# Out-projection ended pair by pair with its weights taken four times, the second product's first loads in idle pages of the x ring, and unit 0's splits placed step by step

## Chip, cores and metric

The kernel runs on one NeuronCore of a Trainium2 chip. The metric is the device time of one execution in microseconds, lower is better. TensorE does the matmuls and transposes, VectorE (DVE) and ScalarE (ACT) the elementwise work, GpSimd (POOL) a few small operations, and SyncE's queue (SP) issues the transfers named here.

## What is computed

A trunk of two layers over 1024 tokens of width 1024. Each layer is a token mixer with a norm and a residual, then a SwiGLU feed-forward with inner width 2816, again with norm and residual. Both parts are wrapped in RMS norms. The mixers (an mLSTM with memory attention in layer 0, sliding-window attention with memory attention in layer 1) are not touched by the change.

```python
def swiglu(h, w_in, w_out):
    gate, up = jnp.split(h @ w_in, 2, axis=-1)
    return (jax.nn.silu(gate) * up) @ w_out

for l in range(DEPTH):
    ...
    mix = jnp.concatenate([main, mo], axis=-1) @ w_out[l]
    x = x + rmsnorm(mix, g_mix_post[l])
    x = x + rmsnorm(swiglu(rmsnorm(x, g_ffn_pre[l]), w_ffn_in[l], w_ffn_out[l]), g_ffn_post[l])
```

## The kernel before

All large products are of float32 accuracy, from three matmuls of reduced operands each. An operand v is split into hi, a rounded copy that ScalarE makes (a cast), and lo = v - hi, which VectorE makes; the product is hi by hi, hi by lo, lo by hi. So each tile of weights costs a load (256 KB for 128x512), a cast and a subtraction before TensorE can use it. The helper `mm` (L177) records every matmul, so almost all matmuls stand under that line; transposes are L184.

**Out-projection** (class `OutProjection`, L500 to 555). The 1024 tokens are eight tiles of 128. `tiles(n, ts)` makes half n (512 columns) of the product for the tiles ts, 8 rows of weights deep; `weights(n)` takes the half's weights into the ring of hi and lo parts (8 buffers of each, raw parts in a ring of 4; L206 to L217). The two halves alternate, since the ring holds one half's weights and a new take fills it as the old one is read: half 0 for tiles 0, 4 and 1, 5, then half 1 for all tiles in pairs, then half 0 again for 2, 6, then 3 and 7 alone. So three takes a layer. A half product is squared on ScalarE for its norm (L242) and multiplied by the gain on VectorE into y (L520). When a tile has both halves, `finish` (L467 to 494) runs as side work: load of the residual xr (L471), sum of squares, r, one scalar_tensor_tensor (STT, L484) that adds the residual, the store of y (L486), squares, a second r, and xn = y * r on ScalarE (L494). Then `absorb` (L317 to 342) transposes xn on TensorE into PSUM, copies it to f (L324), and, when the second tile of a pair (t and t + 4) is there, makes sums sx, sy and splits them into parts named a22, s1, s3 (a11 was made by the first tile).

**First product of the feed-forward** (`ffn_in`). Units (p, g): 11 pairs p of 256 columns, for gate (g = 0) and up (g = 1). Each unit is one 2x2 block product with seven multiplications, Strassen's way: seven steps, each with an operand of the tokens (a11, s1, ...) and one of the weights (b11, t1, ...), summed into three PSUM chains u, c, d. `prep` (L608, L609) splits one weight operand, `evict` (L679 to L704) takes the results out of PSUM, `side` places the splits and loads of the unit that comes next. Unit 0 is done in two halves, for tiles 0, 4, 1, 5 and then 2, 6, 3, 7, since the tokens arrive late; all of its seven weight operands are split ahead of its first half. `operands` (L713 to L725) stores the unit's results, and sums sx and sy of them, to DRAM as the spill `sp`.

**Second product** (`ffn_out`): the same seven steps with 11 pairs each, 77 loads of a token operand from `sp` (L785) and a weight operand (L791) into pages, each split by L799 (cast) and L800 (lo). Loads of steps 0 and 1 stand in the raw ring, of the others in the x ring, which has 5 pages of 128x1024. The generator is entered once, by `then()` after ffn_in's last unit (L762).

**What sets the order.** The elementwise order of VectorE, ScalarE and GpSimd in this stretch is that in which the program records it (a manual schedule). A modelled clock, `line.poll`, decides after which matmul the next piece of side work (`finish`, `absorb`) is recorded. TensorE's and SyncE's orders are set by the scheduler; a queue runs strictly in its order, so an instruction that waits holds up all behind it.

## Time and profile before

| | us |
|---|---|
| median of 3 runs | 2196.94 (2193.93 to 2198.35) |
| the profiled execution's own time | 2195.92 |
| its span in the profile | 2194.1 |
| mean granted TensorE clock | 0.984 of full speed |

The profile is one execution. In it PE is TensorE, DVE VectorE, ACT ScalarE. A timeline row is start, duration and instruction in the form out<-in, and in brackets the time that the engine was idle before it, with what ended the wait. Durations overlap on one engine, so the distance of starts tells how fast a queue goes. Names: po is the out-projection's PSUM tile; fgu, fgc, fgd (gate) and fuu, fuc, fud (up) the first product's chains; fou, foc, fod the second's; pt_mix holds transposes; wout, b11g, t1g and so on are weight operands; so the second product's operands; gx, gy, ux, uy the units' results.

### The profile page before, as it was taken

To read this page: it belongs to the slowest core of one execution; us is meant where nothing else is said; L and a number is where in the kernel's file an instruction comes from. 1 tells how busy PE (TensorE), PEld (TensorE's weight loads), DVE (VectorE), ACT (ScalarE), POOL (GpSimd) and SP (SyncE) were. 2 spreads that over 40 slices of the span, in tenths; PEclk is the share of its full clock that TensorE was granted. 3 is DMA by queue.
4 is the path that set the end of the run, shared out by engine and by line. 5 is a ranking of instruction groups with operands and counts; after the bars stand their busy time and mean duration, and the time that the engine had idled before them with its cause. 6 is when DMAs were issued, how large, how long until landed. Compare 5 with 4: busy or idle time off the path is not lost.

```text
span 2194.1 us, 30716 instructions
## 1 busy us (share of the span) xinstructions
PE 2103.6 (96%) x11011; PEld 1809.0 (82%) x11011; DVE 1284.1 (59%) x2462; ACT 1126.1 (51%) x2429; POOL 131.1 (6%) x245
## 2 busy tenths in 40 slices
PE   7999997989999999899999999999899999989997
PEld 6899986877888888688888998988788888878886
DVE  6331247576675757565585347747757676655556
ACT  5541145576555555344474426647655554534444
POOL 1100032000000000000021021000000000000002
PEclk9999998999999999999999999999999999999998
DMA  6111152253454535466672112025245454447666
GB/s 217 54 30 34 50 172 70 87 173 111 148 171 136 184 134 171 165 216 202 193 251 89 41 35 78 2 78 172 94 138 183 138 171 161 141 155 234 194 192 230
DMA packets 174841, 301.34 MB, mean 137 GB/s; under 512 B 20544, under 2 KB 78432, under 8 KB 174688
## 3 DMA queue, kind: packets, MB, share of 16 engines
q1 hardware_dynamic: 174688, 299.38, 42.0%
q8 instruction: 86, 1.41, 0.3%
q14 instruction: 67, 0.55, 0.1%
HBM read 215.94 MB, written 83.38 MB: 136 GB/s over the span
## 4 chain that ended last, share of the span: by engine, by line
PE 79%; issue 10%; DVE 4%; ACT 3%; DMA 2%; POOL 1%; SPq 0%; POOLq 0%; ACTq 0%; DVEq 0%
PE fuu L177 11%; PE fgu L177 10%; PE fou L177 10%; PE po L177 8%; PE fud L177 5%; PE fod L177 5%; PE fgd L177 5%; PE pb_q L177 3%; PE foc L177 3%; PE fuc L177 3%; PE fgc L177 2%; PE pa_ogm L177 2%; PE pov L177 2%; PE pt_mix L184 1%; PE pb_mq L177 1%
## 5 line engine op out<-in xcount | busy, mean ns | idle before, releaser
L800 DVE TENSOR_TENSOR so_lo<-so,so_hi 128x512 fp32r<-128x512 f32 x300 | 195.9, 689 | 172.9 <-ACT so_hi L799 172.7
L799 ACT CAST so_hi<-so 128x512 fp32r<-128x512 f32 x300 | 173.8, 619 | 211.2 <-PE fou L177 82.3
L177 PE MATMUL po<-wout_hi,f 128*128 128x512 f32 x512 | 161.8, 394 | 6.3 <-DVE f L258 6.3
L177 PE MATMUL fou<-so_hi,so_hi 128*128 128x512 f32 x352 | 138.3, 396 | 11.1 <-ACT so_hi L799 11.1
L177 PE MATMUL fou<-so_lo,so_hi 128*128 128x512 f32 x352 | 138.9, 395 | 3.6 <-DVE so_lo L800 3.6
L177 PE MATMUL fou<-so_hi,so_lo 128*128 128x512 f32 x352 | 138.4, 393 | 0.0
L236 POOL TENSOR_TENSOR r<-v,neghalf 128x1 f32<-128x1 f32 (+1 forms) x76 | 55.9, 746 | 1167.5 <-DVE v L234 977.4
L177 PEld LDWEIGHTS po<-wout_hi,f 128*128 128x128 f32 x512 | 97.1, 190 | 26.6 <-DVE f L258 6.6
L177 PE MATMUL po<-wout_lo,f 128*128 128x512 f32 x256 | 100.5, 393 | 0.0
L177 PEld LDWEIGHTS fou<-so_hi,so_hi 128*128 128x128 f32 x352 | 67.0, 190 | 25.8 <-ACT so_hi L799 11.9
L177 PEld LDWEIGHTS fou<-so_lo,so_hi 128*128 128x128 f32 x352 | 67.0, 190 | 18.9 <-DVE so_lo L800 5.3
L177 PEld LDWEIGHTS fou<-so_hi,so_lo 128*128 128x128 f32 x352 | 66.9, 190 | 13.9
L609 DVE TENSOR_TENSOR t1u_lo<-wu,t1u_hi 128x512 fp32r<-128x512 f32 x22 | 15.2, 692 | 101.6 <-ACT t1u_hi L608 101.6
L598 ACT ACTIVATE wu<-wu,gin 128x256 f32<-128x256 f32 x176 | 73.5, 499 | 1.6 <-DMA wu<-in_w_ffn_in 1.5
L598 ACT ACTIVATE wg<-wg,gin 128x256 f32<-128x256 f32 x176 | 73.2, 499 | 0.0
L177 PE MATMUL pb_q<-w_q_hi,h 128*128 128x384 f32 x256 | 72.4, 346 | 0.0
L177 PE MATMUL fod<-so_hi,so_lo 128*128 128x512 f32 x176 | 68.5, 389 | 0.0
L177 PE MATMUL fod<-so_lo,so_hi 128*128 128x512 f32 x176 | 68.5, 389 | 0.0
L177 PE MATMUL fod<-so_hi,so_hi 128*128 128x512 f32 x176 | 68.5, 389 | 0.0
L177 PE MATMUL pa_v<-wa_v_hi,h 128*128 128x384 f32 x256 | 65.4, 336 | 0.0
L619 DVE TENSOR_TENSOR wo_raw<-wo_raw,wo_raw 128x512 f32<-128x512 f32 x88 | 60.6, 689 | 1.5
L177 PE MATMUL fgd<-f,t1g_hi 128*128 128x512 f32 (+1 forms) x192 | 56.0, 374 | 2.1 <-DVE f L314 2.1
(445 smaller groups left out, 5806.9 us busy)
## 6 DMA issues: line engine op xcount, KB each, us to landing
so<-sp SPq DMA_DIRECT2D x150, 256.0 KB, 3.0
wg<-in_w_ffn_in SPq DMA_DIRECT2D x44, 512.0 KB, 3.8
wu<-in_w_ffn_in SPq DMA_DIRECT2D x44, 512.0 KB, 4.1
wo_raw<-in_w_ffn_out SPq DMA_DIRECT2D x88, 256.0 KB, 3.4
tp<-wo_raw SPq DMA_DIRECT2D x88, 256.0 KB, 3.1
so<-tp SPq DMA_DIRECT2D x88, 256.0 KB, 3.5
so<-in_w_ffn_out SPq DMA_DIRECT2D x62, 256.0 KB, 3.4
wout_raw<-in_w_out SPq DMA_DIRECT2D x48, 256.0 KB, 3.0
```

The source lines that it names most:

```text
L177: pe.matmul(o, lhsT=lhsT, rhs=rhs, start=start, stop=stop, **kw)
L184: pe.transpose(o, src, ident[: src.shape[0], : src.shape[0]])
L236: pool.tensor_tensor(out=r, in0=v, in1=neghalf[:, :width], op=ALU.pow)
L598: act.activation(v, v, AF.Copy, scale=gin[:, l, 4 * i + k : 4 * i + k + 1])
L609: dve.tensor_tensor(out=lo, in0=v, in1=h.bitcast(F32), op=ALU.subtract)
L619: dve.tensor_tensor(out=r[o], in0=r[x_], in1=r[y_], op=ALU.add)
L799: act.copy(h, v)
L800: dve.tensor_tensor(out=lo, in0=v, in1=h.bitcast(F32), op=ALU.subtract)
```

## The change

Five edits.

1. In `absorb`, the second half of f is copied from PSUM by VectorE instead of ScalarE (L324).
2. The parts of a pair's second tile are made in the order s1, s3, a22, not a22, s1, s3.
3. The out-projection's last pairs: half 1 of tiles 2, 6, then half 0 of 2, 6, which ends that pair; then half 0 of 3, 7, and last half 1 of 3 and of 7. Half 1's weights are taken a second time, so there are four takes a layer.
4. In unit 0, three weight operands are split ahead of it, the others one by one, at steps of its first half.
5. The second product's generator is entered three times within the last unit, behind its steps 4, 5 and 6: loads of steps 0 to 2 first, then split 0 and load 3, then split 1 and load 4. All of its loads go to pages of the x ring.

```diff
@@ -321,7 +321,7 @@
                 for i in range(4):
                     k = 4 * j + i
                     flip(pt[:, i * P : (i + 1) * P], xn[:, k * P : (k + 1) * P])
-                act.copy(f[:, j * 512 : (j + 1) * 512], pt)
+                (dve.tensor_copy if j else act.copy)(f[:, j * 512 : (j + 1) * 512], pt)
             if not second:
                 self.first[slot] = f
                 yield 0.5
@@ -335,11 +335,11 @@
             dve.tensor_tensor(out=sx[:, 512:], in0=sx[:, :512], in1=a11, op=ALU.subtract)
             dve.tensor_tensor(out=sy[:, :512], in0=a11, in1=a21, op=ALU.subtract)
             dve.tensor_tensor(out=sy[:, 512:], in0=a12, in1=sx[:, 512:], op=ALU.add)
-            self.parts(slot, "a22", a22, 1)
-            yield 1
             self.parts(slot, "s1", sx, 2)
             yield 1
             self.parts(slot, "s3", sy, 2)
+            yield 1
+            self.parts(slot, "a22", a22, 1)
 
     def token_gemm(outs, acts, w):
 
@@ -547,12 +547,12 @@
             self.tiles(1, (0, 4))
             mixed(3, 7)
             self.tiles(1, (1, 5))
-            self.tiles(1, (2, 6))
-            self.tiles(1, (3, 7), lambda: self.weights(0))
+            self.tiles(1, (2, 6), lambda: self.weights(0))
+            self.tiles(0, (2, 6))
+            self.tiles(0, (3, 7), lambda: self.weights(1))
             early()
-            self.tiles(0, (2, 6))
             for t in (3, 7):
-                self.tiles(0, (t,))
+                self.tiles(1, (t,))
 
 
 
@@ -734,7 +734,7 @@
         ordered.__enter__()
         for u, (p, g) in enumerate(units):
             if u == 0:
-                for _, op in STEPS:
+                for _, op in STEPS[:3]:
                     prep(0, op)
                 need(xo, (0, 4, 1, 5))
             results(u)
@@ -759,8 +759,11 @@
                         line.poll()
                     if slots[1] == 4:
                         side(u, s)
+                    elif s + 3 < len(STEPS):
+                        prep(0, STEPS[s + 3][1])
                     evict(u, s, acc, c0, c1)
-        then()
+                    if u == len(units) - 1 and s >= 4:
+                        then()
         for s in (0, 4, 6):
             operands(NP - 1, s)
         ordered.__exit__(None, None, None)
@@ -777,11 +780,8 @@
         def load(n):
             s, p = steps[n]
             sop, wop = STEPS[s]
-            if n < 2:
-                r = raws[n] = [raw_part(f"so{l}_{n}_{i}") for i in range(2)]
-            else:
-                x_ = xpage(f"so{l}_{n}")
-                r = raws[n] = [x_[:, i * 512 : (i + 1) * 512] for i in range(2)]
+            x_ = xpage(f"so{l}_{n}")
+            r = raws[n] = [x_[:, i * 512 : (i + 1) * 512] for i in range(2)]
             nc.sync.dma_start(out=r[0], in_=sp[p][:, SP.index(sop)])
             if wop in TP:
                 nc.sync.dma_start(out=r[1], in_=tp_[p][:, TP.index(wop)])
@@ -800,9 +800,14 @@
                 dve.tensor_tensor(out=lo, in0=v, in1=h.bitcast(F32), op=ALU.subtract)
                 parts[n] += [h, lo]
 
-        for n in range(2):
+        for n in range(3):
             load(n)
-            split_parts(n)
+        yield
+        split_parts(0)
+        load(3)
+        yield
+        split_parts(1)
+        load(4)
         yield
         gpost = grow(a["g_ffn_post"][l], f"gfpost{l}")
         nxt = open_acts(name) if name else None
@@ -839,13 +844,12 @@
                 dve.tensor_tensor(out=z[:, lo], in0=v, in1=gpost[:, lo], op=ALU.mult)
                 line.run(finish(z, z, ss[t2], t2, src, spill, nxt, f"ffn{l}", nxt is None), nxt and (nxt.name, t2))
 
-        load(2)
         for n, (s, p) in enumerate(steps):
             name, begin = CHAIN[s]
             if p == 0 and begin:
                 for j in range(4):
                     acc[name, j] = ps(f"fo{name}{l}_{j}")
-            if n + 3 < len(steps):
+            if 5 <= n + 3 < len(steps):
                 load(n + 3)
             ah, al, bh, bl = parts.pop(n)
             for j in range(4):
```

VectorE, from layer 0's last unit of the first product into the second. L696 to L704 finish the unit's results, L716 to L723 are the sums of its operands; so_2_0_lo is step 2's token operand. Before:

```order
L696 TENSOR_TENSOR ux_10_8088<-ux_10_8088,gx_10_7930 128x512 x2
L703 TENSOR_TENSOR uy_10_8089<-fuu_10_8090,gy_10_7931 128x512
L704 TENSOR_TENSOR uy_10_8089<-uy_10_8089,gy_10_7931 128x512
L800 TENSOR_TENSOR so_0_0_lo<-so_0_0_raw,so_0_0_hi 128x512
L800 TENSOR_TENSOR so_0_1_lo<-so_0_1_raw,so_0_1_hi 128x512
L800 TENSOR_TENSOR so_1_0_lo<-so_1_0_raw,so_1_0_hi 128x512
L800 TENSOR_TENSOR so_1_1_lo<-so_1_1_raw,so_1_1_hi 128x512
L716 TENSOR_TENSOR sx_10_8234<-uy_10_8089 128x512
...
L717 TENSOR_TENSOR sx_10_8234<-sx_10_8234,ux_10_8088 128x512
L722 TENSOR_TENSOR sy_10_8237<-ux_10_8088,uy_10_8089 128x512
...
L800 TENSOR_TENSOR so_2_0_lo<-so_2_8268,so_2_0_hi 128x512
L800 TENSOR_TENSOR so_2_1_lo<-so_2_8268,so_2_1_hi 128x512
```

and with the change:

```order
L696 TENSOR_TENSOR ux_10_8136<-ux_10_8136,gx_10_7978 128x512 x2
L800 TENSOR_TENSOR so_0_0_lo<-so_0_8225,so_0_0_hi 128x512
L800 TENSOR_TENSOR so_0_1_lo<-so_0_8225,so_0_1_hi 128x512
L703 TENSOR_TENSOR uy_10_8137<-fuu_10_8138,gy_10_7979 128x512
L704 TENSOR_TENSOR uy_10_8137<-uy_10_8137,gy_10_7979 128x512
L800 TENSOR_TENSOR so_1_0_lo<-so_1_8228,so_1_0_hi 128x512
L800 TENSOR_TENSOR so_1_1_lo<-so_1_8228,so_1_1_hi 128x512
L716 TENSOR_TENSOR sx_10_8289<-uy_10_8137 128x512
L800 TENSOR_TENSOR so_2_0_lo<-so_2_8231,so_2_0_hi 128x512
L717 TENSOR_TENSOR sx_10_8289<-sx_10_8289,ux_10_8136 128x512
L722 TENSOR_TENSOR sy_10_8292<-ux_10_8136,uy_10_8137 128x512
...
L800 TENSOR_TENSOR so_2_1_lo<-so_2_8231,so_2_1_hi 128x512
```

Step 0's two lo now stand ahead of the uy operations, and step 1's behind them; step 2's are mixed with the sums sx and sy, where they stood behind all of them.

SyncE over the same place. L713 to L725 are the stores of a unit's results and sums, sp_10 those of the last pair. Before:

```order
L713 DMA sp_10_4380<-ux_10_8088 128x1024
...
L714 DMA sp_10_4380<-uy_10_8089 128x512
...
L214 DMA w_kv_raw<-in_w_kv 128x512 x2
L721 DMA sp_10_4380<-sx_10_8234 128x1024
L725 DMA sp_10_4380<-sy_10_8237 128x1024
L785 DMA so_2_8268<-sp_2_4372 128x512
L791 DMA so_2_8268<-in_w_ffn_out 128x512
L785 DMA so_3_8275<-sp_3_4373 128x512
```

and with the change, one unit earlier, behind the stores of pair 9:

```order
L721 DMA sp_9_4517<-sx_9_8007 128x1024
L785 DMA so_0_8225<-sp_0_4508 128x512
L791 DMA so_0_8225<-in_w_ffn_out 128x512
L725 DMA sp_9_4517<-sy_9_8096 128x1024
L785 DMA so_1_8228<-sp_1_4509 128x512
L791 DMA so_1_8228<-in_w_ffn_out 128x512
L785 DMA so_2_8231<-sp_2_4510 128x512
L791 DMA so_2_8231<-in_w_ffn_out 128x512
L785 DMA so_3_8257<-sp_3_4511 128x512
L791 DMA so_3_8257<-in_w_ffn_out 128x512
L785 DMA so_4_8284<-sp_4_4512 128x512
L791 DMA so_4_8284<-in_w_ffn_out 128x512
```

The loads of steps 2 to 4 stood behind the stores of sx_10 and sy_10; now all loads up to step 4 stand ahead of every store of pair 10.

VectorE at the end of layer 0's out-projection, where y_3 and y_7 are the last two tiles and b11g_0_lo is what unit 0's first product needs. Before:

```order
L520 TENSOR_TENSOR y_3_4356<-po_0_3_4470,gmp_3632 128x512
...
L609 TENSOR_TENSOR b11g_0_lo<-wg_0_0_4392,b11g_0_hi 128x512
...
L609 TENSOR_TENSOR b21g_0_lo<-wg_0_1_4394,b21g_0_hi 128x512
L609 TENSOR_TENSOR t2g_0_lo<-t_raw,t2g_0_hi 128x512
L609 TENSOR_TENSOR t1g_0_lo<-t_raw,t1g_0_hi 128x512
L609 TENSOR_TENSOR t3g_0_lo<-t_raw,t3g_0_hi 128x512
L609 TENSOR_TENSOR b22g_0_lo<-wg_0_1_4394,b22g_0_hi 128x512
L520 TENSOR_TENSOR y_7_4363<-po_0_7_4513,gmp_3632 128x512
```

and with the change:

```order
L324 COPY f_mix_2_4573<-pt_mix_2_1_4580 128x512
L324 COPY f_mix_6_4586<-pt_mix_6_1_4593 128x512
L334 TENSOR_TENSOR sx_mix_6_4599<-f_mix_6_4586 128x512
L314 TENSOR_TENSOR f_3637<-f_mix_2_4573,f_3637 128x2x512
...
L337 TENSOR_TENSOR sy_mix_6_4600<-f_mix_2_4573,sx_mix_6_4599 128x512
L520 TENSOR_TENSOR y_3_4494<-po_1_3_4550,gmp_3632 128x512
L314 TENSOR_TENSOR f_3637<-sx_mix_6_4599,f_3637 128x2x512
L314 TENSOR_TENSOR f_3637<-sy_mix_6_4600,f_3637 128x2x512
L314 TENSOR_TENSOR f_3637<-f_mix_6_4586,f_3637 128x512
...
L520 TENSOR_TENSOR y_7_4501<-po_1_7_4619,gmp_3632 128x512
...
L609 TENSOR_TENSOR b11g_0_lo<-wg_0_0_4530,b11g_0_hi 128x512
```

b11g_0_lo stood behind y_3's last product and ahead of y_7's. Now it stands behind both, and behind the copies, sums and splits of tiles 2 and 6, which stood behind it. A stretch ahead of these rows, the lo of the fourth take (wout_1_0 to wout_1_7) are new.

## Rows read from the trace of the kernel before

**Rows 1.** The page's line of busy time by engine (us, share of the span, instructions), and the shares of the chain that ended last.

```profile
PE 2103.6 (96%) x11011; PEld 1809.0 (82%) x11011; DVE 1284.1 (59%) x2462; ACT 1126.1 (51%) x2429; POOL 131.1 (6%) x245
...
PE 79%; issue 10%; DVE 4%; ACT 3%; DMA 2%; POOL 1%; SPq 0%; POOLq 0%; ACTq 0%; DVEq 0%
```

**Rows 2.** Windows: stretch (us), its length, busy us and instructions of PE, PEld, DVE, ACT and POOL, granted clock, DMA share, GB/s. The first two are layer 0's out-projection and unit 0, the third its way into the second product; the fourth and fifth are layer 1's unit 0 and its way into the second product.

```profile
376.25:472.35 96.10, 96.10 (x449) 80.37 (x449) 56.97 (x103) 52.92 (x105) 6.90 (x13) 0.98 0.30 101
472.35:511.64 39.29, 29.22 (x205) 27.53 (x203) 25.91 (x41) 30.29 (x56) 2.55 (x3) 0.91 0.34 116
913.90:933.50 19.60, 11.12 (x37) 8.09 (x36) 12.16 (x20) 4.98 (x9) 2.79 (x35) 0.83 0.89 287
1520.40:1559.70 39.30, 29.00 (x203) 27.27 (x203) 25.95 (x41) 30.12 (x55) 2.57 (x3) 0.91 0.31 103
1962.26:1978.85 16.59, 10.40 (x38) 7.58 (x36) 11.01 (x18) 4.98 (x9) 0.00 (x0) 0.90 0.81 283
```

**Rows 3.** Timeline of TensorE over the second product's first steps, layer 0 and, from 1962.26, layer 1: start, duration, instruction, and in brackets the idle time before it and what ended it.

```profile
913.90 1.07 PE L177 MATMUL fou<-so_hi,so_hi 128*128 128x512 f32 x4
...
916.85 0.50 PE L177 MATMUL fou<-so_lo,so_hi 128*128 128x512 f32 x1 [1.88 <-DVE so_lo L800]
...
928.27 0.80 PE L177 MATMUL fou<-so_hi,so_hi 128*128 128x512 f32 x1 [6.60 <-ACT so_hi L799]
...
930.44 0.63 PE L177 MATMUL fou<-so_lo,so_hi 128*128 128x512 f32 x1
...
930.87 0.63 PE L177 MATMUL fou<-so_hi,so_lo 128*128 128x512 f32 x1
...
933.50 0.39 PE L177 MATMUL fou<-so_hi,so_hi 128*128 128x512 f32 x1
...
933.73 0.40 PE L177 MATMUL fou<-so_lo,so_hi 128*128 128x512 f32 x1
...
1962.26 1.07 PE L177 MATMUL fou<-so_hi,so_hi 128*128 128x512 f32 x4
...
1965.01 0.50 PE L177 MATMUL fou<-so_lo,so_hi 128*128 128x512 f32 x1 [1.68 <-DVE so_lo L800]
...
1974.34 0.80 PE L177 MATMUL fou<-so_hi,so_hi 128*128 128x512 f32 x1 [4.50 <-ACT so_hi L799]
...
1978.85 0.40 PE L177 MATMUL fou<-so_hi,so_hi 128*128 128x512 f32 x1
```

**Rows 4.** Timeline of VectorE, SyncE's queue (SPq) and ScalarE in the same stretch of layer 0.

```profile
911.99 1.28 DVE L696 TENSOR_TENSOR ux<-ux,gx 128x512 f32<-128x512 f32 x2
...
914.10 0.69 DVE L703 TENSOR_TENSOR uy<-fuu,gy 128x512 f32<-128x512 f32 x1 [0.83 <-PE fuu L177]
...
914.71 0.68 DVE L704 TENSOR_TENSOR uy<-uy,gy 128x512 f32<-128x512 f32 x1
...
915.31 2.89 DVE L800 TENSOR_TENSOR so_lo<-so_raw,so_hi 128x512 fp32r<-128x512 f32 x4
...
920.18 0.68 DVE L723 TENSOR_TENSOR sy<-ux,sx 128x512 f32<-128x512 f32 x1
...
920.89 0.33 SPq L725 DMA_DIRECT2D sp<-sy  x1
...
921.27 0.99 SPq L785 DMA_DIRECT2D so<-sp  x1
...
926.69 0.62 ACT L799 CAST so_hi<-so 128x512 fp32r<-128x512 f32 x1 [13.51 <-DMA so<-sp]
```

**Rows 5.** The chain that ended last, pieces in order of time (start, us, what), out-projection and unit 0 of layer 0.

```profile
429.53 1.75 PE pt_mix L184 x16
...
494.57 1.05 ACT xn_mix L494
...
495.67 1.54 PE pt_mix L184 x8
...
501.56 3.20 ACT wu L598 x8
```

**Rows 6.** Timeline of TensorE, transposes of unit 0 (x16 are tiles 2 and 6, x8 tile 7).

```profile
478.97 3.58 PE L184 MATMUL pt_mix<-ident,xn_mix 128*128 128x128 f32 x16 [2.15 <-ACT xn_mix L494]
...
495.67 1.52 PE L184 MATMUL pt_mix<-ident,xn_mix 128*128 128x128 f32 x8 [3.87 <-ACT xn_mix L494]
```

**Rows 7.** Timeline of VectorE from the end of the out-projection into unit 0, layer 0.

```profile
469.58 0.69 DVE L609 TENSOR_TENSOR b11g_lo<-wg,b11g_hi 128x512 fp32r<-128x512 f32 x1 [0.36 <-ACT b11g_hi L608]
...
471.75 0.68 DVE L609 TENSOR_TENSOR t2g_lo<-t_raw,t2g_hi 128x512 fp32r<-128x512 f32 x1
...
472.35 0.68 DVE L609 TENSOR_TENSOR t1g_lo<-t_raw,t1g_hi 128x512 fp32r<-128x512 f32 x1
...
475.36 1.28 DVE L484 SCALAR_TENSOR_TENSOR y<-y,r,xr_mix 128x1024 f32<-128x1024 f32 x1
...
488.43 1.22 DVE L314 TENSOR_TENSOR f<-sx_mix,f 128x1024 fp32r<-128x1024 f32 x1
```

**Rows 8.** Timeline of ScalarE, the table load for silu in unit 0, layer 0.

```profile
491.04 1.28 ACT L693 ACT_TABLE_LOAD   x1
```

**Rows 9.** Group of instructions by line and form: count | busy us, mean ns of one | idle before.

```profile
L1387 DVE COPY pT<-pt 128x512 f32<-128x512 f32 x21 | 14.4, 687 | 0.0
```

**Rows 10.** The tile wout_raw, all 48 loads of 256 KB.

```profile
DMA to landing us min/median/max: 2.4/3.0/5.6
```


## Prediction

> **What bounds it now.** The page's busy line and its chain of waits come first: TensorE is busy 96% of the span, and 79% of the chain that ended last is its matmuls [rows 1]. So only places where TensorE waits, or runs at its lower clock, can give time back. The windows show the two kinds of place that the edits touch [rows 2]. While the out-projection runs, TensorE is busy in all of its 96.10 us and VectorE in 56.97. In feed-forward unit 0 (472.35 to 511.64 in layer 0) TensorE is busy 29.22 of 39.29 us, and layer 1's stretch reads the same (29.00 of 39.30). From the last unit into the second product (913.90 to 933.50) it is busy 11.12 of 19.60 us at a granted clock of 0.83; layer 1's loses a little less, at 0.90.
>
> **Into the second product.** TensorE's timeline has it step by step [rows 3]. In layer 0 step 0's first four matmuls start at 913.90. Then it waits 1.88 us for so_lo, and before step 2 it waits 6.60 us for a cast. After that the matmuls stand 0.43 us apart (930.44, 930.87) where later ones stand 0.23 apart (933.50, 933.73): of the clock's two levels the lower, 1.2 GHz, after that idle time. A step is 12 matmuls at 0.227, so 2.72 us, and step 3 could start at 913.90 + 3 x 2.72 = 922.06. It starts at 933.50: 11.4 us lost. Layer 1 waits 1.68 and 4.50 us and starts step 3 at 1978.85 where 1962.26 + 8.16 = 1970.42 was due: 8.4 us lost.
>
> The causes stand on VectorE, ScalarE and SyncE [rows 4]. VectorE can make so_lo (915.31) only after the two uy operations at 914.10 and 914.71. Step 2's load is issued at 921.27, behind the sy store at 920.89, which waits for VectorE's sy (920.18); the cast follows its landing at 926.69.
>
> The change puts steps 0 to 2 into idle pages of the x ring, so SyncE has all the loads up to step 4 ahead of the last unit's stores, a unit of some 30 us earlier. They cost SyncE issue slots in a stretch where it waits on data, and nothing on the path. VectorE now does so_0's two lo ahead of uy: 911.99 + 2 x 0.6 puts them at 913.3 to 914.5, in time. Behind them stand uy twice, so_1's two (the second done at about 917.2, needed at 916.6 + 0.3), sx, so_2's first, three sums, so_2's second. At 0.60 us apart (471.75 to 472.35) [rows 7] the last is done near 921.0, needed near 919.9. I count two waits of 0.3 and 1.1 us, 1.4 a layer, too short to bring the lower clock, as the 1.88 us wait did not. The gain is 11.4 - 1.4 = **10.0** in layer 0 and 8.4 - 1.4 = **7.0** in layer 1. Bounds: nothing left of either loss (19.8), or a second wait as long as layer 0's first in each (16.0 would be left of 19.8 at 1.9 each). What is late next is step 5, which needs the page that so_2's second lo frees: issued about 921, landed by 925, needed at 928.
>
> **Out-projection and unit 0.** TensorE does the same matmuls. The 16 transposes of tiles 2 and 6, 1.75 us [rows 5], move from unit 0 into the out-projection, which ends at 474.1 instead of 472.35, and no longer wait there (2.15 us at 478.97) [rows 6]. That is what the new order buys: pair 2, 6 is finished one pair earlier, so tiles 3 and 7 alone are left behind the last matmul.
>
> It pays with a fourth take of the weights: 8 loads, 8 casts on ScalarE, 8 subtractions on VectorE; ScalarE loses as many f copies (8 a layer), VectorE gains them. A VectorE copy out of PSUM lasts 0.687 us [rows 9], like the other half-width operations. Rows 4 to 7 of this take use buffers that rows 0 to 3 must leave, and their loads stand on SyncE behind the stores of y_2 and y_6, whose STT runs at about 457; so I issue them at 457.7. At the median landing of 3.0 us [rows 10] they land at 460.7, are cast at 461.6 and subtracted at 462.25. TensorE wants row 4 when it reaches tile 3 alone: 474.1 less two tiles of 24 matmuls (5.44 each) and the 1.75 is 461.5, and four rows of 0.68 later is 464.2. So the take is covered by 2 us.
>
> But VectorE has no gap from 461.65: 20 half-width operations (four lo of the take, four t_raw, four y products, two f copies, four sums, and lo of t and f), three full-width lo at 1.2 [rows 7] and small ones, 12.1 + 3.5 + 0.4 = 16.0, stand ahead of and with b11g_lo, which ends at 477.7; before, it started at 469.58. TensorE gets a **new wait of 2.6 us** or so behind the out-projection's last matmul (with no lower clock if it goes as after 2.15 us; after 3.87 us it came, and would cost at most some 2 us, in matmuls whose end then still lies ahead of tile 3's f). From 477.7 tile 7's work queues behind splits: b21, t2, y_3's STT (1.2), t1, t3, gx, b22, y_7's STT, about 7.0 us on VectorE to 484.65; then on ScalarE y_7's square 1.2 and xn_3 1.05 (each a pass over 1,024 columns, as the xn at 494.57), gy 0.3, the table load 1.28 [rows 8], four silu, a copy and a cast 2.7, and xn_7 1.05: 492.25. In the kernel before, xn_7 ends at 495.6 (494.57 + 1.05) [rows 5]. What follows is the same work: transposes, f, sums, casts, the eight gains of wu (3.20 at 501.56), and unit 0's last matmuls, 16 us to 511.64; the copy that VectorE takes and the new order s1, s3, a22 make it shorter by 0.2. So 3.4 + 0.2 = **3.6 us a layer**, 7.2 in all. Bounds: TensorE's whole idle time in unit 0, 10.1 us a layer [rows 2], and, with the loads landing in the longest row's 5.6 us, 1.0.
>
> **Sum.** The profiled execution took 2195.9 us; 2195.9 - 17.0 - 7.2 = 2171.7. The median of the runs lies 1.0 above it, so the prediction is **2172**. About 0.2%, 4.4 us, is what a measurement can tell from no change.
>
> **Rivals.**
> A. The fourth take lands late. For it: its loads wait in SyncE's order for two stores, and the DMA share is 0.30 there, 0.34 in unit 0 with landing times from 2.4 to 5.6 us [rows 2, 10]. Every us past 3.0 moves VectorE's queue, so unit 0 gives 1.0 a layer or slightly less than nothing: 2195.9 - 17.0 - 2.0, so 2177 to 2182. The Trainium skill, "DMA: Bandwidth & Descriptors", adds a mechanism in "Latency and other measured facts": access latency of memory rises from 0.2 us to about 2 us under high load. By that, as an estimate from the page, landing would come 1.8 us later and the total near 2175; the spread of the rows here agrees with a load effect, without saying which of its parts it is.
> B. Unit 0 gives much more. VectorE's queue is as short as I have priced it, but splits that are placed step by step may let y_7's STT and square pass, so that TensorE loses only about 2 of its 10.1 us: 8 a layer, 2195.9 - 17.0 - 16.0 = 2163. Against it: the order of VectorE and ScalarE is fixed as written, and there the splits do stand ahead of tile 7.
> C. The change does not do what it says: the pages are not idle, the early loads wait for their last readers, and the second product still starts late. Then only unit 0's 7.2 is left: 2189. Against it: the pages' last readers are the stores of unit 9's sums, and they stand right ahead of the loads on SyncE.
> D. Slower: tiles 3 and 7 starve. If the take's rows 4 to 7 are held behind the y_6 store, which needs the STT, its r and its xr load, TensorE stops inside the out-projection, where it never waits now. To eat 17.0 this must cost 8.5 a layer after unit 0's gain of 3.6, so 12.1 a layer: the loads would have to land 14 us later than 460.7, with the 2 us of cover. At 16 us a layer, with the lower clock behind it, the total is near 2205. Against it: the longest landing is 5.6 us, and no operation ahead of the store is priced over 1.3.
>
> **Chances.** The forecast (2166 to 2177) has 0.52, A 0.20, B 0.18, C 0.05, D 0.05. A range of 2160 to 2187 holds forecast, A, B and the bounds of the transition, and leaves out C, D and the outer ends: about 0.15. Faster by over 0.2% is all but D and a corner of C: 0.94; within 0.2%: 0.02; slower: 0.04.
>
> **What would show it.** Right: no wait of 4 us or more ahead of fou's first three steps in either layer, that stretch near 9.5 us at clock 1.0 instead of 19.60 and 16.59, step 3 near 922 after its step 0 at 914; the transposes of tiles 2 and 6 inside the out-projection; a new wait of 2 to 3 us ahead of the first fgu, ended by b11g_lo on VectorE; unit 0 from the end of the out-projection's matmuls some 34 us long instead of 39.29. Wrong: a wait of TensorE for wout_lo or wout_hi in the last half products (A, or D if it is long); no wait ahead of the first fgu, or a far shorter unit 0 (B); a wait on so_hi as before (C). A wait further into the second product, at step 5, would be the transition's loss moved on, not removed.

## The result, and the profile after

The changed kernel takes 2184.78 us (median of 5 runs, 2183.79 to 2189.07) against 2196.94: a ratio of 0.995, 95% interval 0.9933 to 0.9968. It is faster, by 12.2 us where 24.9 were forecast. The profiled execution is the longest of the five, 2189.07 us with a span of 2187.3.

The executions differ by some 5 us in stretches that no edit touches (the first out-projection matmul starts at 373.5 to 378.5 us over the profiles of this study), so the stages are compared, each from its own first matmul:

| stretch, us | before | after | after - before |
|---|---|---|---|
| out-projection, layer 0 / 1 | 96.10 / 94.28 | 99.09 / 96.86 | +2.99 / +2.58 |
| unit 0, layer 0 / 1 | 39.29 / 39.46 | 40.74 / 40.49 | +1.45 / +1.03 |
| second product's first matmul to layer 1's input projection (its first pb_mq matmul) | 290.35 | 279.72 | -10.6 |
| second product's first matmul to the end, layer 1 | 218.05 | 210.03 | -8.0 |

So the way into the second product gave 18.6, a little more than forecast, and out-projection with unit 0, forecast to give 3.6 a layer, took 4.4 and 3.6. By the medians the loss is 18.6 - 12.2 = 6.4 over both layers, not 8.0; the stages are those of one execution. (Layer 1's unit 0 ends at 1559.90 in the kernel before; its window in [rows 2] stops 0.2 us short of that.)

Windows of the changed kernel, same columns as [rows 2]: layer 0's out-projection, its unit 0, the second product's first 8.6 us, then layer 1's unit 0 and its second product.

```profile
378.24:477.33 99.09, 98.50 (x465) 81.75 (x465) 65.25 (x116) 58.97 (x113) 8.73 (x12) 0.98 0.37 123
477.33:518.07 40.74, 30.30 (x189) 28.80 (x187) 26.95 (x45) 24.90 (x48) 4.59 (x4) 0.79 0.31 103
920.36:929.00 8.64, 8.29 (x36) 6.24 (x35) 8.64 (x14) 1.74 (x3) 3.07 (x35) 1.00 0.77 210
1520.24:1560.73 40.49, 29.68 (x187) 28.28 (x188) 27.78 (x46) 25.66 (x49) 4.62 (x4) 0.83 0.28 91
1962.97:1971.60 8.63, 8.60 (x38) 6.64 (x37) 8.63 (x15) 1.75 (x3) 0.00 (x0) 1.00 0.58 215
```

The second product now starts at full clock, where [rows 2] had 0.83 and 0.90. Unit 0 is no shorter, and its clock fell from 0.91 to 0.79.

TensorE and SyncE at the second product of the changed kernel, layer 0:

```profile
920.36 0.84 PE L177 MATMUL fou<-so_hi,so_hi 128*128 128x512 f32 x3
...
921.04 0.44 PE L177 MATMUL fou<-so_lo,so_hi 128*128 128x512 f32 x1
...
927.40 0.50 PE L177 MATMUL fou<-so_lo,so_hi 128*128 128x512 f32 x1 [0.35 <-DVE so_lo L800]
```

```profile
886.09 0.42 SPq L785 DMA_DIRECT2D so<-sp  x1
...
895.02 0.32 SPq L725 DMA_DIRECT2D sp<-sy  x1
895.38 0.43 SPq L785 DMA_DIRECT2D so<-sp  x1
...
899.10 0.43 SPq L791 DMA_DIRECT2D so<-in_w_ffn_out  x1
```

Against [rows 3, 4]: the waits of 1.88 and 6.60 are gone, all that is left is 0.35; the loads up to step 4 are issued by 899.5, over 20 us ahead of their use, where step 2's went out 7 us behind step 0's start. In layer 1 no wait is left there.

TensorE in layer 0's unit 0, the rows that answer to [rows 6]:

```profile
480.03 0.50 PE L177 MATMUL fgd<-f,t1g_hi 128*128 128x256 f32 x2 [2.07 <-ACT t1g_hi L608]
...
482.83 0.58 PE L177 MATMUL fgu<-f,b11g_lo 128*128 128x256 f32 x1 [2.30 <-DVE b11g_lo L609]
...
498.25 1.97 PE L184 MATMUL pt_mix<-ident,xn_mix 128*128 128x128 f32 x8 [2.84 <-ACT xn_mix L494]
...
508.80 0.80 PE L177 MATMUL fgu<-f,t2g_hi 128*128 128x256 f32 x2 [2.35 <-ACT gx L679]
```

The forecast wait for b11g_lo is there, 5.5 us behind unit 0's first matmul at 477.33 (TensorE fills 1.1 of it with hi products that need no lo). Behind t2 at 508.80 matmuls run at the lower clock. How the three engines come to this stands in the queues of SyncE, ScalarE and VectorE:

```profile
443.04 2.09 SPq L214 DMA_DIRECT2D wout_raw<-in_w_out  x4
445.18 2.05 SPq L588 DMA_DIRECT2D wg<-in_w_ffn_in  x2
...
459.62 1.52 SPq L486 DMA_DIRECT2D x<-y  x2
461.42 2.58 SPq L214 DMA_DIRECT2D wout_raw<-in_w_out  x4
```

```profile
451.66 0.91 ACT L598 ACTIVATE wg<-wg,gin 128x256 f32<-128x256 f32 x2 [3.31 <-DMA wg<-in_w_ffn_in]
452.48 1.03 ACT L313 CAST f<-sx_mix 128x1024 fp32r<-128x1024 f32 x1
...
473.86 1.57 ACT L313 CAST f<-f_mix 128x1024 fp32r<-128x1024 f32 x2 [3.00 <-DVE f_mix L324]
```

```profile
466.13 0.69 DVE L217 TENSOR_TENSOR wout_lo<-wout_raw,wout_hi 128x512 fp32r<-128x512 f32 x1 [2.48 <-ACT wout_hi L216]
...
472.81 1.28 DVE L324 COPY f_mix<-pt_mix 128x512 f32<-128x512 f32 x2
...
482.10 0.68 DVE L609 TENSOR_TENSOR b11g_lo<-wg,b11g_hi 128x512 fp32r<-128x512 f32 x1
```

The kernel before issued the two halves of wg so:

```profile
430.77 0.38 SPq L588 DMA_DIRECT2D wg<-in_w_ffn_in  x1
...
443.23 0.82 SPq L588 DMA_DIRECT2D wg<-in_w_ffn_in  x1
```

Read down: unit 0's gate weights wg stand on SyncE behind the first four of the take's loads. Their first half goes out at 445.18 instead of 430.77, and the halves land 6.4 and 7.4 us after issue instead of 4.3 and 4.8. ScalarE waits 3.31 us for them with the casts of f queued behind, so the y products and y_2's and y_6's store come late (459.62), and with them rows 4 to 7 of the take (461.42). VectorE gets to row 4's lo at 466.13, to the copies of f at 472.81 (ScalarE waits 3.00 us for them), and to b11g_lo at 482.10.

### The profile page after: what moved, and what is told of

Its sections match the earlier page's. It is cut to its first block, busy times and chain, and to the rows that moved or that the text cites. A ratio compares the mean times of both kernels' runs of the same rounds, so it can differ in the third digit from the quotient of the medians.

```text
span 2187.3 us, 30823 instructions
## 1 busy us (share of the span) xinstructions
PE 2107.8 (96%) x11011; PEld 1813.2 (83%) x11011; DVE 1303.1 (60%) x2494; ACT 1126.1 (51%) x2429; POOL 138.7 (6%) x245
## 4 chain that ended last, share of the span: by engine, by line
PE 76%; issue 10%; DVE 5%; ACT 3%; DMA 3%; POOL 2%; SPq 0%; POOLq 0%; ACTq 0%; DVEq 0%
PE fuu L177 11%; PE fgu L177 11%; PE fou L177 10%; PE fud L177 5%; PE fod L177 5%; PE fgd L177 5%; PE po L177 4%; PE pb_q L177 3%; PE foc L177 3%; PE fuc L177 3%; PE fgc L177 3%; PE pov L177 2%; PE pa_ogm L177 2%; PE pt L184 1%; PE pb_mq L177 1%
## 5 line engine op out<-in xcount | busy, mean ns | idle before, releaser
L800 DVE TENSOR_TENSOR so_lo<-so,so_hi 128x512 fp32r<-128x512 f32 x308 | 201.1, 689 | 157.0 <-ACT so_hi L799 157.0
L799 ACT CAST so_hi<-so 128x512 fp32r<-128x512 f32 x308 | 178.2, 619 | 196.8 <-PE fou L177 73.8
L177 PE MATMUL fou<-so_lo,so_hi 128*128 128x512 f32 x352 | 137.4, 390 | 0.4 <-DVE so_lo L800 0.3
L236 POOL TENSOR_TENSOR r<-v,neghalf 128x1 f32<-128x1 f32 (+1 forms) x76 | 63.3, 843 | 1148.4 <-DVE v L234 971.8
L177 PE MATMUL fou<-so_hi,so_hi 128*128 128x512 f32 x352 | 135.3, 390 | 0.0
L177 PEld LDWEIGHTS fou<-so_lo,so_hi 128*128 128x128 f32 x352 | 66.1, 188 | 15.4 <-DVE so_lo L800 1.9
L217 DVE TENSOR_TENSOR wout_lo<-wout_raw,wout_hi 128x512 fp32r<-128x512 f32 x64 | 44.7, 715 | 36.7 <-ACT wout_hi L216 36.6
L177 PE MATMUL fgu<-f,t2g_hi 128*128 128x512 f32 (+1 forms) x192 | 58.3, 388 | 4.7 <-ACT gx L679 4.7
```

What stands on the lines that cost most here:

```text
L177: pe.matmul(o, lhsT=lhsT, rhs=rhs, start=start, stop=stop, **kw)
L217: dve.tensor_tensor(out=l, in0=raw, in1=h.bitcast(F32), op=ALU.subtract)
L236: pool.tensor_tensor(out=r, in0=v, in1=neghalf[:, :width], op=ALU.pow)
L799: act.copy(h, v)
L800: dve.tensor_tensor(out=lo, in0=v, in1=h.bitcast(F32), op=ALU.subtract)
```

## Experiments

The table gives each run's time (median, or that of one run), and for layers 0 and 1: out-projection and unit 0 together; from unit 0's first matmul to its first b11g_lo; from t2 in its second half to its end, which is 6.57 at full clock. "Early loads" is the second product's part of the change. The stages are read from one profiled execution of each kernel. One kernel was profiled twice (early loads and splits by step): its sums differ by 1.2 and 0.7 us, so differences of that size are not told apart here. The profile of "all but part order" is of an execution of 2187.55 us, 5.2 above its median.

| run | us | out-proj. + unit 0 | to b11g_lo | t2 to end |
|---|---|---|---|---|
| before | 2196.94 | 135.4 / 133.7 | 0.2 / 0.2 | 6.6 / 6.6 |
| after | 2184.78 | 139.8 / 137.4 | 5.5 / 6.3 | 9.3 / 8.0 |
| early loads alone | 2174.79 | 135.4 / 133.4 | 0.2 / 0.2 | 6.6 / 6.6 |
| all but early loads | 2203.12 | 137.9 / 137.9 | 5.2 / 5.9 | 8.1 / 9.3 |
| early + part order | 2182.51, one | 138.1 / 136.5 | 0.2 / 0.2 | 6.6 / 6.6 |
| early + VectorE copy | 2177.62, one | 135.3 / 133.7 | 0.2 / 0.2 | 6.6 / 6.6 |
| early + splits by step | 2172.93, one | 133.4 / 130.7 | 0.2 / 0.2 | 6.6 / 6.6 |
| the same again | 2173.54 | 134.6 / 131.4 | 0.2 / 0.2 | 8.1 / 6.6 |
| early + fourth take | 2177.34, one | 133.6 / 133.1 | 3.0 / 3.8 | 6.6 / 6.6 |
| all but fourth take | 2180.47 | 138.1 / 135.2 | 0.2 / 0.2 | 8.0 / 8.1 |
| all but part order | 2182.31 | 139.2 / 136.8 | 5.2 / 6.0 | 8.1 / 7.9 |
| all but VectorE copy | 2177.00, one | 135.7 / 133.2 | 3.7 / 4.5 | 6.6 / 6.6 |
| all but splits by step | 2186.49, one | 138.4 / 136.8 | 4.6 / 5.2 | 8.1 / 8.0 |
| all, wg early | 2179.39 | 135.0 / 135.8 | 3.2 / 4.7 | 8.1 / 9.2 |
| that, old part order | 2173.98 | 133.0 / 132.1 | 3.2 / 4.1 | 6.6 / 6.6 |
| take, splits by step | 2179.29, one | 135.3 / 133.7 | 3.7 / 4.1 | 6.6 / 7.9 |
| that, wg early | 2173.41 | 132.5 / 130.9 | 2.7 / 2.6 | 6.6 / 6.6 |

**Early loads alone.** The hunks of `then` and `ffn_out`, on the kernel before:

```diff
-        then()
+                    if u == len(units) - 1 and s >= 4:
+                        then()
...
-        for n in range(2):
+        for n in range(3):
             load(n)
-            split_parts(n)
+        yield
+        split_parts(0)
+        load(3)
...
```

> The kernel before with the early loads and split-by-split entry of the second product alone; the out-projection, the f copies, the part order and unit 0's splits stay as before. Theory (the gain is all here): in the two profiles the stretch from the second product's first matmul on is 10.6 us shorter in layer 0 and 8.0 us in layer 1, so 2196.9 - 18.6 = 2178, below the whole change. Prediction as made: 2196.9 - 17.0 = 2180. Rival (this part gains only about 12, and the out-projection nothing either way): 2185, the same as the whole change.

2174.79 us, ratio 0.9904 (0.9891 to 0.9918); from the second product's first matmul 279.74 and 210.04 us, as in the whole change. This part alone beats the whole change, so the rest of it costs: 10.0 us by the medians, 8.4 by the stages.

**All but the early loads.** The same hunks undone in the changed kernel (`then()` behind the loop, loads 0 and 1 in the raw ring).

> The change without the early loads of the second product: fourth take, new pair order, f copies on VectorE, parts s1, s3, a22, splits step by step. Prediction as made: 2196.9 - 7.2 = 2190. Theory from the two profiles (out-projection and unit 0 together 4.4 us longer in layer 0, 3.6 in layer 1): 2205, slower than before.

2203.12 us, ratio 1.0033 (1.0023 to 1.0044): slower than before. The theory's side; the forecast of a gain falls.

**Loads early, splits not.**

```diff
-                    if u == len(units) - 1 and s >= 4:
+                    if u == len(units) - 1 and s == 4:
                         then()
+        then()
+        then()
         for s in (0, 4, 6):
```

> The kernel before with the second product's first loads early, but its first two splits behind the last unit's evictions, as before. To be read from the second product's first matmul to layer 1's input projection (290.4 us before, 279.7 with loads and splits moved) and to the end (218.1 and 210.0). Theory: the loads give the 4.5 to 6.6 us waits and the lower clock, the splits' place only the first wait of 1.7 to 1.9, so 281.5 and 211.8. Rival: splits behind the evictions hold the first steps back as before, whatever the loads do: 286 or more and 215.

280.89 and 211.57 us: 9.5 and 6.5 of the gain are the loads', 1.1 and 1.5 the splits'. The first wait is back unchanged, the others stay away:

```profile
915.64 0.50 PE L177 MATMUL fou<-so_lo,so_hi 128*128 128x512 f32 x1 [1.88 <-DVE so_lo L800]
...
1954.40 0.50 PE L177 MATMUL fou<-so_lo,so_hi 128*128 128x512 f32 x1 [1.68 <-DVE so_lo L800]
```

**All but the fourth take.** The hunk of `OutProjection.all` undone:

```diff
-            self.tiles(1, (2, 6), lambda: self.weights(0))
-            self.tiles(0, (2, 6))
-            self.tiles(0, (3, 7), lambda: self.weights(1))
+            self.tiles(1, (2, 6))
+            self.tiles(1, (3, 7), lambda: self.weights(0))
             early()
...
```

> The whole change with the out-projection's order and its three takes of the weights as before. Theory A (the fourth take and what stands behind its loads, wg's among them, is what made unit 0 late): the loss of 8 us goes, 2177 or less. Theory B (VectorE's f copies, or the splits that now stand in unit 0's own first half, are the loss): still 2183 or more.

2180.47 (0.9926, 0.9914 to 0.9939): between the two theories. Without the take, 1.8 and 2.1 us come back; the three other edits, on the early loads, cost 2.7 and 1.8.

**Single edits on the early loads**: part order, copy, splits, take. The first three (the fourth is the diff above the other way round):

```diff
-            self.parts(slot, "a22", a22, 1)
-            yield 1
             self.parts(slot, "s1", sx, 2)
...
+            self.parts(slot, "a22", a22, 1)
```

```diff
-                act.copy(f[:, j * 512 : (j + 1) * 512], pt)
+                (dve.tensor_copy if j else act.copy)(f[:, j * 512 : (j + 1) * 512], pt)
```

```diff
-                for _, op in STEPS:
+                for _, op in STEPS[:3]:
...
+                    elif s + 3 < len(STEPS):
+                        prep(0, STEPS[s + 3][1])
```

> The early loads of the second product (as in the first run of this study) with only the part order s1, s3, a22 added. To be read in unit 0's stretch, 39.5 and 39.1 us without it and 42.1 and 41.0 with all three of part order, VectorE copy and splits step by step. Theory: a22's cast now stands last on ScalarE, ahead of wu's eight gains and the copy of gx, so TensorE's wait ahead of t2 grows from 1.24 to about 2.3 us and TensorE falls to the lower clock behind it: 1.5 us longer in each layer. Rival: the same casts in another order cost nothing, 39.5 and 39.1.

> The early loads of the second product with only the VectorE copy of f's second half added. Theory: tile 7's two copies run beside each other, so unit 0 is some 0.5 us shorter in each layer (39.0 and 38.6). Rival: VectorE's queue is what unit 0 waits for, so the copies make it longer by up to 1 us.

> The early loads of the second product with only the splits of unit 0 step by step added. Theory: b22's cast stands behind other work on ScalarE, so TensorE waits in unit 0's first half where it did not (the 3.17 us ahead of b22 in the run with three takes), and unit 0 is 1 to 2.5 us longer in each layer. Rival: that wait lies ahead of one for tile 3 that shrinks as much, and unit 0 stays at 39.5 and 39.1.

> The early loads of the second product and the fourth take with its pair order, nothing else (f copies on ScalarE, parts a22, s1, s3, all splits ahead of unit 0). To be read over out-projection and unit 0 together: 135.4 and 133.4 us with three takes, 139.8 and 137.4 with all edits. Theory (the take with wg's load behind it delays b11g_lo; part order costs 2.7 more and step-by-step splits give 2.7 back): the take alone is 4 us longer in each layer, 139 and 137. Rival (the pair order gains by itself, as predicted, and only the part order spoils it): 132 and 130.

The part order costs 2.7 and 3.1 us a layer. The wait ahead of t2 does grow, from 1.24 to 2.35 us, but the loss is not where the theory put it: t2 to the end stays at 6.6. It comes earlier, on ScalarE behind tiles 2 and 6; first the run with the new order, then the one without:

```profile
485.65 1.04 ACT L313 CAST f<-sx_mix 128x1024 fp32r<-128x1024 f32 x1 [2.35 <-DVE sx_mix L335]
486.60 0.36 ACT L685 COPY gy<-fgd 128x256 f32<-128x256 f32 x1
486.86 1.06 ACT L242 ACTIVATE junk<-y 128x1024 bf16<-128x1024 f32 x1
```

```profile
481.90 0.63 ACT L313 CAST f<-f_mix 128x512 fp32r<-128x512 f32 x1
482.42 0.39 ACT L685 COPY gy<-fgd 128x256 f32<-128x256 f32 x1
482.69 1.08 ACT L242 ACTIVATE junk<-y 128x1024 bf16<-128x1024 f32 x1
...
484.36 1.05 ACT L313 CAST f<-sx_mix 128x1024 fp32r<-128x1024 f32 x1 [0.51 <-DVE sx_mix L335]
```

With sx first, ScalarE sits 2.35 us for a sum that VectorE has not made, and y_7's square (junk<-y) waits behind it; in the old order a22's cast, the copy of gy and the square fill that time. The VectorE copy does nothing by itself (-0.1 and +0.3). Splits by step gain 2.0 and 2.7 (0.8 and 2.0 when run again, where layer 0's end ran at the lower clock): the theory of a loss is wrong. The fourth take alone gains 1.8 and 0.3 us in these stages (0.7 in layer 1 against the kernel before), less than its rival said but on its side: the forecast wait is there (3.0 and 3.8 us to b11g_lo), and what stands behind gives more than it takes. Its one execution, 2177.34 us, is not faster than the early loads alone.

**Whole change, one edit undone**: part order, copy, splits, each of the three diffs above taken back.

> The whole change with the parts in their old order a22, s1, s3, and wg's load where the change has it. Read over out-projection and unit 0 together: 139.8 and 137.4 us with all edits, 133.0 and 132.1 with wg early and the old order. Theory P (the part order is the loss; wg's late landing costs only because ScalarE and VectorE already wait for each other): 133 to 135 and 131 to 133, time 2175 to 2178. Theory W (wg's late landing is a loss of its own): 136.5 to 138 and 135 to 136, time 2181 to 2183.

> The whole change with both halves of f copied by ScalarE, as before. Theory (VectorE has no gap ahead of b11g_lo, so 1.2 us a pair of tiles off its queue come off the wait): 1 to 2 us shorter in each layer than 139.8 and 137.4. Rival (alone the copies cost and gave nothing, and ScalarE waits either way): within 0.7 of 139.8 and 137.4.

> The whole change with unit 0's seven splits all ahead of it, as before. Theory (splits step by step gained 0.8 to 2.7 us a layer by themselves, since four splits no longer stand ahead of tile 7's work): 1 to 3 us longer in each layer than 139.8 and 137.4. Rival (with the new part order they cost, as three takes with it read 42.1 in unit 0): 1 to 2 us shorter.

Each edit is worth something else here than alone. The part order costs 0.6 a layer instead of 3, too little to tell from nothing (2182.31 us, 0.9939, 0.9922 to 0.9955; by the medians 1.2 a layer). Theory P falls; theory W's time is met, its stage times are not. Splits by step no longer gain: they read 1.5 and 0.6 longer, and 1.2 of the 1.5 is the lower clock from t2 on. And the copy, free by itself, costs 4.2 and 4.1, more than its theory. Of layer 0's 4.2, b11g_lo takes 1.8 and the lower clock 2.7 (0.4 is given back elsewhere). The last stretch of unit 0, first in the changed kernel, then without the copy, with the t2 row of the latter:

```profile
498.25:507.50 9.25, 7.32 (x44) 6.72 (x44) 6.22 (x8) 5.42 (x10) 0.00 (x0) 0.84 0.01 2
507.50:518.07 10.57, 9.27 (x52) 8.98 (x52) 5.75 (x10) 4.93 (x13) 0.00 (x0) 0.68 0.00 0
```

```profile
493.92:504.28 10.36, 8.01 (x44) 7.81 (x44) 5.53 (x7) 7.29 (x15) 0.00 (x0) 0.72 0.01 2
504.28:510.86 6.58, 6.58 (x51) 6.34 (x52) 5.57 (x10) 3.22 (x9) 0.00 (x0) 1.00 0.00 0
```

```profile
504.28 0.51 PE L177 MATMUL fgu<-f,t2g_hi 128*128 128x256 f32 x2 [2.35 <-ACT gx L679]
```

The same 2.35 us wait for ScalarE's copy gx stands ahead of t2 in both (the changed kernel's windows are cut within it, 1.3 us ahead of t2). Without the copy the low clock lies ahead of that wait (0.72), where it costs nothing that shows, and t2 to the end runs at 1.00; with it the order is the other way round, 0.84 and 0.68, and low clock there is paid in full. That the copy is what moves the low clock is not shown.

**wg early.** `ffn_in` yields behind `gained(0)` (the eight ScalarE operations that multiply wg by the norm's gain), and the out-projection enters it one pair earlier:

```diff
-            self.tiles(1, (2, 6), lambda: self.weights(0))
+            self.tiles(1, (2, 6), lambda: (early(), self.weights(0)))
...
         load(0)
         gained(0)
+        yield
```

> The whole change, with unit 0's gate weights wg loaded and gained one pair earlier, ahead of the half-0 weights instead of behind eight wout loads. In the changed kernel ScalarE waits 3.31 us for wg at 451.66 and all behind it on ScalarE and VectorE is late. Theory A1 (wg's late landing is what starts the delay): b11g_lo 2 to 3 us earlier in both layers, 2179 to 2181. Theory A2 (the take itself, with VectorE's 16 more operations, is the delay, and wg's wait is covered): no change, 2184 to 2186.

2179.39 us (0.9918, 0.9905 to 0.9932), 4.9 and 1.6 us a layer, b11g_lo 2.3 and 1.6 us earlier: A1, with layer 1 short of its 2 to 3. (The edit puts wg's load ahead of the take's in the queue and one pair of tiles earlier in the program; the run does not tell the two apart.) ScalarE's wait of 3.31 us for wg is gone, and of the 3.00 us for the copies 0.57 is left. With the old part order on top, and then also with the copies back on ScalarE:

> The whole change with wg loaded early, and the parts in their old order a22, s1, s3. Theory: ScalarE no longer waits for sx with a square or a copy queued behind it, so unit 0 is 1.5 to 3 us shorter in each layer than with the new order (36.9 and 39.7): 2175 to 2176. Rival (with four takes VectorE's queue ahead of b11g_lo sets the start, and the order of parts no longer counts): 2179.

> The whole change without the VectorE copies and without the new part order: fourth take with pair order, splits step by step, early loads, wg's load where the change has it. Read over out-projection and unit 0 together. Theory (the copies are the loss, since ScalarE waits for VectorE and VectorE for ScalarE; wg's late landing alone is covered): below the 135.7 and 133.2 of the run with only the copies undone, by the part order's 0.6 to 2.7: 133 to 135 and 131 to 132.6. Rival (the late wg still costs, copies or not): 135.5 and 133 or more.

> The same with wg loaded and gained one pair early. Theory (every loss found is taken out): 131 to 132 in out-projection and unit 0 of both layers, 2174.0 - 2 = 2172, the fastest of this study. Rival (the out-projection's end is bound by the chain of tile 7 and what is left of VectorE's queue): as the run with copies and early wg, 133.0 and 132.1, 2174.

2173.98 (0.9903, 0.9889 to 0.9917): with wg early the part order costs 2.0 and 3.7, of which 1.5 and 2.6 are the lower clock from t2 on. The pair without copies and part order, with wg late and early, reads 135.3 / 133.7 and 132.5 / 130.9: the late wg costs 2.8 a layer by itself (in layer 1, 1.3 of it from t2 on), so the theory that it is covered is wrong and its rival right. The same rows price the copy again, with the old part order: with wg late 3.9 and 3.1 (139.2 / 136.8 against 135.3 / 133.7), with wg early 0.4 and 1.2 (133.0 / 132.1 against 132.5 / 130.9). So most of its cost needs the late wg. The last kernel has the shortest unit 0 of all, 34.3 and 34.8 us (windows of both layers), with the wait for b11g_lo at 1.77:

```profile
475.53:509.85 34.32, 25.58 (x189) 24.11 (x188) 22.47 (x39) 23.16 (x47) 4.59 (x4) 0.95 0.34 117
1510.29:1545.10 34.81, 25.60 (x189) 24.14 (x187) 22.47 (x39) 23.13 (x47) 4.62 (x4) 0.95 0.29 98
```

```profile
478.18 0.39 PE L177 MATMUL fgu<-f,b11g_lo 128*128 128x256 f32 x1 [1.77 <-DVE b11g_lo L609]
```

**The two gaining edits, timed again.** Early loads and splits by step.

> The early loads of the second product and the splits of unit 0 step by step, nothing else: the two edits that gained by themselves, timed. Theory: unit 0 is 2.7 us shorter in each layer than with the early loads alone, so 2174.8 - 5.4 = 2169.4, faster than both kernels. Rival (the first look's 2.7 is taken back in unit 1 or in the out-projection): 2174 to 2175.

2173.54 us (0.9903, 0.9887 to 0.9919); the last kernel above 2173.41 (0.9903, 0.9887 to 0.992). Early loads alone have 0.9904. All three beat both kernels; their times do not tell them apart. The stage sums put the other two 2.8 to 5.4 us over both layers below the early loads alone; between those two they decide nothing, since the kernel that was profiled twice reads 133.4 / 130.7 and 134.6 / 131.4 and the last kernel 132.5 / 130.9. So the fourth take, even with wg early, shows no gain in time over splits by step without it.

**Evictions ahead of side work in unit 0**, on the early loads.

```diff
+                    if u == 0 and slots[1] == 4:
+                        evict(u, s, acc, c0, c1)
                     if slots[1] == 4:
                         side(u, s)
-                    evict(u, s, acc, c0, c1)
+                    if u or slots[1] < 4:
+                        evict(u, s, acc, c0, c1)
```

> The early loads of the second product, and in unit 0's second half the evictions recorded ahead of the side work (wu's eight gains, next splits) of the same step. Theory (the copy of gx behind 3.3 us of gains on ScalarE is what holds TensorE ahead of t2): that wait, 1.24 us, goes, unit 0 is about 38 us, and the time is 2174.8 - 2.4 = 2172. Rival (the gains are only pushed behind and unit 1 waits for wu instead): the same, 2174 to 2176.

2177.16 (0.9917, 0.9901 to 0.9934). Unit 0 is 1.2 and 0.8 us shorter, and the units behind it 0.8 and 1.0 longer, with waits for wu's splits that were not there: the rival, 1 us beyond its range.

```profile
504.89 0.73 PE L177 MATMUL fuu<-f,b11u_hi 128*128 128x512 f32 x2 [0.44 <-ACT b11u_hi L608]
...
515.71 0.73 PE L177 MATMUL fud<-f,t1u_hi 128*128 128x512 f32 x2 [0.76 <-ACT t1u_hi L608]
```

## Why the prediction was right in one half and wrong in the other

The terms forecast, 17.0 and 7.2, add up to 24.2 us and to 2172.7 by the prediction's own sum; it was written down as 2172.

**Into the second product: right.** 17.0 us forecast, 18.6 measured, by the mechanism named. The two short waits, 1.4 a layer, came out at 0.35 and none. Rival C falls, and what was late next, step 5, made no wait.

**Out-projection and unit 0: wrong in sign.** In layer 0, forecast and measured differ by 8.0 us (-3.6 and +4.4), and each term has its share, against a start that lies 2.0 us later in this profile:

| term, us | forecast | measured | without copy and part order, wg early |
|---|---|---|---|
| out-projection longer by | 1.75 | 2.99 | 2.1 |
| unit 0's start to b11g_lo | 3.6 | 5.5 | 2.7 |
| b11g_lo to tile 7's transposes | 14.6 | 15.4 | 15.8 |
| transposes to the end | 15.8 | 19.8 | 15.9 |

1. "I issue them at 457.7" failed. On the forecast's scale rows 4 to 7 were issued at 459.4 and row 4's lo made at 464.1, not 461.65: 1.7 us by the issue, 0.8 by landing and cast. The step priced what the take's loads stand behind, not what stands behind the take: wg's load, whose first half went out at 430.77 before and at 445.18 now, with ScalarE waiting for it. In the last kernel, with wg early, the issue is 80.8 us behind the out-projection's start, against 81.4 forecast, and b11g_lo, the table's last column, is within 1 us of the forecast. The 2 us of cover for row 4 were used up: TensorE waited 0.22 and 0.37 us for the take's lo, half of what the out-projection is longer than forecast. The length of VectorE's queue was right: 16.0 forecast, 16.6 from 466.13 to 482.78.
2. "A VectorE copy ... like the other half-width operations" failed: priced as its own 0.6 us in the queue. Behind the take's lo it also keeps ScalarE, which waits 3.00 us for it, and with the clock it costs 4.2 a layer. Alone it costs nothing, with wg early 0.4 and 1.2; the price of an edit depended on which engine had slack at that place.
3. The lower clock's "at most some 2 us, in matmuls whose end then still lies ahead of tile 3's f" failed. Its premise, no lower clock "if it goes as after 2.15 us", misread [rows 6]: there the 16 transposes take 3.24 us at a granted clock of 0.52, where those at 429.37 take 1.67. In the changed kernel it came behind the wait for b11g_lo as well (windows as in [rows 2], the kernel before first):

```profile
478.97:482.21 3.24, 3.24 (x17) 3.24 (x17) 0.31 (x1) 2.63 (x4) 0.70 (x1) 0.52 1.02 369
```

```profile
482.83:487.27 4.44, 4.44 (x21) 4.44 (x21) 3.26 (x6) 1.85 (x4) 2.09 (x2) 0.50 0.91 274
```

   That it would cost nothing there was right as far as the runs show: b11g_lo to tile 7's transposes take 15.4 us here and 15.3 with wg early, where that stretch of layer 0 runs at a clock of 1.00. But it came again in unit 0's last matmuls, where nothing covers it and the sum had no term: 2.7 and 1.4 us.
4. "The copy that VectorE takes and the new order s1, s3, a22 make it shorter by 0.2" failed by its second half: the order costs 2.7 and 3.1 on the early loads, 2.0 and 3.7 with wg early, and in the whole change 0.6, which is within what two profiles of one kernel differ by.

Whether ending pair by pair gains is only in part shown. Alone, with its fourth take, it gives 1.8 and 0.3 us in the stages. With wg early and splits by step it gives 2.9 a layer, near the forecast's 3.6, but splits by step give 0.8 to 2.7 of that without it. The take with wg early and without the splits was not run. Rivals B and D were not reached: no unit 0 gained 8, and TensorE's waits for the take's lo stayed at 0.22 and 0.37 us. Rival A had the mechanism, a late take that moves VectorE's queue, with a loss too small. The take's eight loads landed 4.3 us (median) after issue, and rows 4 to 7 after 3.9 to 4.5; the forecast's 3.0 is the median of all 48 loads before, of which the last four of layer 0 already took 4.7. The 1.8 us that the prediction estimated from the Trainium skill, "DMA: Bandwidth & Descriptors", section "Latency and other measured facts", is more than rows 4 to 7 lost against 3.0 (1.0 in the median) and less than wg's two loads lost (2.1 and 2.6). No run tells access latency from queueing here.

Not settled: why the same waits bring the lower clock ahead of t2 in one kernel and behind it in another, and so how much of the copy's and the part order's cost from t2 on is theirs.

## What to carry to other kernels

When a load is added to an in-order queue, follow the next load of every other consumer behind it: here the one that cost 2.8 us a layer, wg's, was not the one that the change was about. Edits that move work between two engines that wait for each other have no price of their own; measure them in the company they will have, both added alone and taken out of the whole. A hoisted load into buffers that are idle anyway was worth more than all the reordering, and its price could be read from the waits of the trace before.

## What the runs showed of the hardware

A wait of the same length, 2.35 us ahead of t2, was followed by 6.58 us of matmuls at a granted clock of 1.00 in one kernel, and by 9.27 us, in a stretch at 0.68, in another; in the first the clock had been at 0.72 over the 10.4 us ahead, in the second at 0.84 over 9.25 us. The kernel that was profiled twice (early loads, splits by step) shows it without any edit: behind waits of 1.23 and 1.22 us, layer 0's stretch from t2 to the end took 6.58 us at 1.00 in one execution and 8.07 at 0.79 in the other, with the clock at 0.82 and 0.84 from tile 7's transposes to t2:

```profile
495.38:504.92 9.54, 7.21 (x45) 6.81 (x45) 5.46 (x7) 7.41 (x15) 0.00 (x0) 0.82 0.01 2
504.92:511.50 6.58, 6.58 (x52) 6.34 (x53) 5.58 (x10) 3.21 (x9) 0.00 (x0) 1.00 0.00 0
```

```profile
491.95:501.79 9.84, 7.14 (x45) 6.73 (x45) 5.46 (x7) 7.40 (x15) 0.00 (x0) 0.84 0.01 2
501.79:509.86 8.07, 8.07 (x52) 7.85 (x52) 5.75 (x10) 3.62 (x9) 0.00 (x0) 0.79 0.00 0
```

So neither the idle time just ahead nor the mean clock ahead of it told by itself which of the two levels (1.2 and 2.4 GHz) followed.
